# A macaron layer in split fp32: when blocks are fetched, where their splits stand in each queue, and who makes a few sums

## The chip, the cores and the metric

The kernel runs on one core of a Trainium2 chip. The metric is device time in microseconds of one execution. The five engines have queues of their own: TensorE (PE: matmuls, transposes), VectorE (DVE), ScalarE (ACT), GpSimd (POOL) and SyncE (SP). SyncE issues most loads and stores, GpSimd the DMAs that add to their destination.

## The reference

One layer, T = 1024 positions, width D = 1024, F = 2816:

```python
x = x + 0.5 * swiglu(rmsnorm(x, ffn1_norm), ffn1_w_in, ffn1_w_out)
x = x + hybrid_mixer(rmsnorm(x, mix_norm), ...)
x = x + 0.5 * swiglu(rmsnorm(x, ffn2_norm), ffn2_w_in, ffn2_w_out)
return rmsnorm(x, final_norm)

def swiglu(h, w_in, w_out):
    gate, up = split(h @ w_in, 2)
    return (silu(gate) * up) @ w_out
# mixer
za, zb, zg = split(h @ w_in, [2 * A, 2 * A + 3 * B])
u, v = split(gelu(za), 2)
v = einsum('hqp,bcphd->bcqhd', w_s, chunks_of_128(rmsnorm(v, sgu_norm))) + b_s
y_a = (u * v) @ w_proj_a
gate_b, gate_c, xb = split(zb, 3)
y_b = (gate_b * short_conv(gate_c * xb, conv_w)) @ w_proj_b     # width 3, by channel
return (sigmoid(g_a) * y_a + sigmoid(g_b) * y_b) @ w_out
```

All of it is float32.

## The kernel before

**Products.** Activations lie with features on the partitions and 512 positions (half the sequence, b = 0, 1) in a tile. Every float32 operand is split into a high part, rounded by a copy on ScalarE, and a low part, src - high on VectorE (`parts`, L87); a product of two operands is three matmuls: high x high, low x high and high x low. Over this lies a scheme with seven instead of eight block products: two output tiles (i = 0, 1) by two halves of the positions, the inner dimension cut in two parts of n tiles (n = 4, in short chunks 3 or 2). `group` makes one such unit: 84 matmuls of 128x512 for n = 4, in the order of products 1, 7, 6, 2, 5, 3, 4 (for n < 4: 1, 7, 6, 2, 5, 4, 3), with ScalarE copies t, u between them (L392), by which VectorE forms the four outputs, and `use` consumes these. `after(i)` is called behind product i and holds other work that shall stand there. `whole_terms` makes plain products, at the start and in two other groups.

**Names.** t1h, t1l ... t7h, t7l are the high and low parts of the seven sums of an activation block (`places`); wh and wl the parts of weights, wr the raw weights. Each weight of a group needs sums too: s2 = wr - wr and others by VectorE (L250, L251), for some weights by accumulating DMAs from GpSimd (`add_to`, L95); `make_ready`, `fetch_until` and `take` run through the list `plan` of all weights, some units ahead of the products. `fourth_sum` splits one of a weight's sums behind a ScalarE copy. gu, o, v, u, cx, gb, gg, ya and yb are the PSUM banks of the products (hidden layer in, layer out, the mixer's parts).

**Stages.** (1) x is loaded and transposed by feature (xT, `by_feature`), scaled by the norm's gain into hr and split; x itself is copied out to DRAM (xd). (2) FFN1: 22 gu groups; finished tiles go to DRAM as seven sums (`Shelf`, g and ts). (3) `out_chunks`: the chunks of FFN1 (4, 4 and 3 tiles twice) against the out weights, four o groups each, added to xd by DMA, the last chunk with the sum in SBUF (xl) and the squares for the next norm (`unhurried` holds these steps back). (4) Mixer: v groups, u groups with sgu (v's norm, `norm_v`; spatial product, `gate_heads`), cx/gb with the convolution, gg (gates), ya, yb, out. (5) FFN2 in the same way, with chunks of 4, 3 and 2 and four tiles (R) left over for (6): plain products o<-wah,gh with the final RMSNorm by token.

**Blocks from DRAM.** A `Shelved` block is fetched back from its shelf, one sum after another (`fetch`: n DMAs into a tile gr or mr, one for each k). Its constructor issues three fetches at once; each `make(i)` splits one sum and issues the next fetch. `last_group` calls `make` in its `after`, one product each, so the next chunk's block is split while the present chunk's last group runs.

**Order.** The scheduler of the Tile framework sets the order on each engine from priorities and the program's order; `tc.high_priority`, `tc.issue_after` and `issue_behind` (an edge without a semaphore) shift single instructions, and an instruction under `tc.keep_in_program_order` stays in the order of the code.

## Time and profile before

| | |
|---|---|
| median of three runs | 2173.31 us (2171.51, 2173.31, 4320.59) |
| profiled execution | 2174.83 us, span 2173.0 |
| TensorE busy | 2111.4 us, 97%, 9374 instructions, mean granted clock 0.99 |
| VectorE, ScalarE, GpSimd busy | 1367.6 (63%), 925.3 (43%), 420.5 (19%) |
| DMA | 435.98 MB, mean 201 GB/s |
| chain that ended last | PE 76%, DVE 7%, DMA 7%, issue 5%, ACT 4% |

The span runs from the first to the last instruction of the profiled execution; its own time is 1.8 us more. Of the run of twice the length there is no profile. Busy shares are means over all stages. The chain is the sequence of work that ended last, followed back from the end.

### The profile page before, as it was taken

To read this page: it belongs to the slowest core of one execution; us is meant where nothing else is said; L and a number is where in the kernel's file an instruction comes from. 1 tells how busy PE (TensorE), PEld (TensorE's weight loads), DVE (VectorE), ACT (ScalarE), POOL (GpSimd) and SP (SyncE) were. 2 spreads that over 40 slices of the span, in tenths; PEclk is the share of its full clock that TensorE was granted. 3 is DMA by queue.
4 is the path that set the end of the run, shared out by engine and by line. 5 is a ranking of instruction groups with operands and counts; after the bars stand their busy time and mean duration, and the time that the engine had idled before them with its cause. 6 is when DMAs were issued, how large, how long until landed. Compare 5 with 4: busy or idle time off the path is not lost.

```text
span 2173.0 us, 27092 instructions
## 1 busy us (share of the span) xinstructions
PE 2111.4 (97%) x9374; PEld 1737.5 (80%) x9374; DVE 1367.6 (63%) x1930; ACT 925.3 (43%) x1350; POOL 420.5 (19%) x486
## 2 busy tenths in 40 slices
PE   7999999999999989999999999999999999999987
PEld 6788888877877878888888888778888888888866
DVE  5855655676477446776654568587755655576666
ACT  5533333355366553222233535356433333354443
POOL 2011111112222111111111101212111111112313
PEclk8999999999999999999999999999999999999999
DMA  8487777979899646897798799867787777988962
GB/s 266 126 199 185 176 193 177 264 221 242 186 239 225 155 106 166 215 255 179 169 262 198 214 290 300 194 178 191 176 206 176 183 196 173 257 237 196 191 185 78
DMA packets 451247, 435.98 MB, mean 201 GB/s; under 512 B 26860, under 2 KB 313636, under 8 KB 451108
## 3 DMA queue, kind: packets, MB, share of 16 engines
q1 hardware_dynamic: 385604, 315.20, 45.4%
q0 software_dynamic: 65504, 119.04, 33.6%
q8 instruction: 73, 1.20, 0.2%
q14 instruction: 66, 0.54, 0.1%
HBM read 235.43 MB, written 100.66 MB: 155 GB/s over the span
## 4 chain that ended last, share of the span: by engine, by line
PE 76%; DVE 7%; DMA 7%; issue 5%; ACT 4%; SPq 1%; POOL 1%; DVEq 0%; POOLq 0%; ACTq 0%
PE gu L83 36%; PE o L83 14%; PE cx L83 7%; PE gg L83 7%; PE gb L83 4%; PE u L83 3%; PE v L83 2%; PE ya L83 2%; DMA gr<-g 1%; DMA wr<-in_ffn_w_out_dram 1%; DVE wl L87 1%; PE sgu L83 1%; PE yb L83 1%; DMA gr<-gd 1%; DMA wr<-wr 1%
## 5 line engine op out<-in xcount | busy, mean ns | idle before, releaser
L87 DVE TENSOR_TENSOR wl<-wr,wh 128x1024 fp32r<-128x1024 f32 (+3 forms) x420 | 441.5, 1054 | 524.9 <-ACT wh L87 516.7
L95 POOL DMA_DIRECT2D wr<-wr x342 | 297.2, 922 | 1489.2 <-DVE wl L87 705.2
L87 ACT CAST wh<-wr 128x1024 fp32r<-128x1024 f32 (+3 forms) x420 | 385.5, 921 | 338.4 <-PE gu L83 102.6
L392 ACT COPY u<-gu 128x512 f32<-128x512 f32 x82 | 47.9, 584 | 188.2 <-PE gu L83 188.2
L760 ACT ACTIVATE gu<-gu 128x512 f32<-128x512 f32 x88 | 55.0, 630 | 114.9 <-DVE gu L601 110.6
L99 DVE SCALAR_TENSOR_TENSOR gu<-gu,u 128x512 f32<-128x512 f32 x82 | 56.4, 688 | 46.7 <-PE gu L83 45.2
L601 DVE TENSOR_TENSOR gu<-gu,rb 128x512 f32<-128x512 f32 x120 | 78.9, 685 | 0.0
L95 POOL DMA_DIRECT2D xd<-o x64 | 56.5, 952 | 103.5 <-DVE o L99 35.3
L392 ACT COPY u<-o 128x512 f32<-128x512 f32 x54 | 31.4, 582 | 84.2 <-PE o L83 81.7
L83 PE MATMUL gu<-t1h,wh 128*128 128x512 f32 x180 | 50.5, 393 | 9.0 <-ACT t1h L87 9.0
L83 PE MATMUL gu<-t2l,wh 128*128 128x512 f32 x180 | 56.8, 390 | 1.6 <-DVE t2l L87 1.6
L83 PE MATMUL gu<-t2h,wh 128*128 128x512 f32 x180 | 57.5, 394 | 0.0
L763 DVE SCALAR_TENSOR_TENSOR gu<-gu,gu 128x512 f32<-128x512 f32 x88 | 57.2, 685 | 0.0
L83 PE MATMUL gu<-t2h,wl 128*128 128x512 f32 x180 | 56.7, 389 | 0.0
L392 ACT COPY t<-gu 128x512 f32<-128x512 f32 x41 | 24.1, 588 | 70.8 <-PE gu L83 70.8
L83 PE MATMUL gu<-t3h,wh 128*128 128x512 f32 x180 | 50.4, 392 | 1.6 <-ACT u L392 1.6
L83 PE MATMUL gu<-t5h,wh 128*128 128x512 f32 x180 | 50.4, 391 | 0.0
L83 PE MATMUL gu<-t1l,wh 128*128 128x512 f32 x180 | 50.2, 390 | 0.0
L83 PE MATMUL gu<-t3l,wh 128*128 128x512 f32 x180 | 50.1, 389 | 0.0
L83 PE MATMUL gu<-t1h,wl 128*128 128x512 f32 x180 | 50.1, 389 | 0.0
L83 PE MATMUL gu<-t5l,wh 128*128 128x512 f32 x180 | 50.1, 389 | 0.0
L83 PE MATMUL gu<-t3h,wl 128*128 128x512 f32 x180 | 50.1, 389 | 0.0
(630 smaller groups left out, 5122.8 us busy)
## 6 DMA issues: line engine op xcount, KB each, us to landing
wr<-wr POOLq DMA_DIRECT2D x318, 256.0 KB, 5.2
wr<-in_ffn_w_in_dram SPq DMA_DIRECT2D x258, 256.0 KB, 4.4
wr<-in_w_in_dram SPq DMA_DIRECT2D x166, 256.0 KB, 4.3
gr<-g SPq DMA_DIRECT2D x140, 256.0 KB, 5.5
g<-ts SPq DMA_DIRECT2D x80, 256.0 KB, 5.2
xd<-o POOLq DMA_DIRECT2D x64, 256.0 KB, 5.8
g<-gu SPq DMA_DIRECT2D x60, 256.0 KB, 4.8
wr<-in_ffn_w_out_dram SPq DMA_DIRECT2D x48, 256.0 KB, 4.4
```

Source lines behind the costliest of these rows:

```text
L83: return nc.tensor.matmul(ps, l, r, start=start, stop=stop, skip_group_check=more)
L87: return nc.scalar.copy(hi, src), nc.vector.tensor_tensor(lo, src, hi.bitcast(F32), ALU.subtract)
L95: nc.gpsimd.dma_start(dst, src, accum_op=ALU.add)
L99: nc.vector.scalar_tensor_tensor(dst, a, -1.0, b, ALU.mult, ALU.subtract)
L392: return nc.scalar.copy(*args)
L601: nc.vector.tensor_tensor(dst, dst, rb, ALU.mult)
L760: nc.scalar.activation(s, s, AF.Silu)
L763: nc.vector.scalar_tensor_tensor(s, s, 0.5, u, ALU.mult, ALU.mult)
```

## The change

- Start: ScalarE's table is loaded by a small copy at the top. Scaling (hr) and x copies are shared between ScalarE and VectorE, t1 and t2 are split in chunks of two tiles, and under `pin` the instructions stay in the code's order; the first half of group f = 0 is written out.
- `Shelved` issues no fetch when it is made; the callers call `fetch` once per group in the three groups ahead.
- Edges: the casts of blocks in `Shelved.make` get an edge behind the newest ScalarE copy u or t, and the low parts of sums 2, 3 and 4 one behind the newest low part of a weight. `unhurried` hands out four steps at a time at two places. u3 has no tile of its own.
- Short chunks (n < 4): one of the sums of a weight (s3, y + x) by VectorE; the same kind of edit for ya/yb: at d = 2 the sum with yb by VectorE.
- v's squares: half in the last v group, half in pairs in the first u group; `flush_v`, `norm_v` and the first `gate_heads` stand behind other products.
- End: remaining weights are fetched and split earlier, copies of xT are shared by ScalarE and VectorE.

```diff
     def parts(hi, lo, src):
-        return nc.scalar.copy(hi, src), nc.vector.tensor_tensor(lo, src, hi.bitcast(F32), ALU.subtract)
+        return pin(nc.scalar.copy(hi, src)), pin(nc.vector.tensor_tensor(lo, src, hi.bitcast(F32), ALU.subtract))
+    pinned = []
+    def pin(ins):
+        return tc.keep_in_program_order(ins) if pinned else ins
@@ make_ready
-                        parts(hi[:, :, :sz], lo[:, :, :sz], src[:, :, :sz])
+                        made = parts(hi[:, :, :sz], lo[:, :, :sz], src[:, :, :sz])
+                    newest_low[:] = [made[1]]
+                    if e == 2:
+                        issue_behind(made[0], newest_gain[0])
...
-                        add_to(y_[:, 0, :sz], x_[:, 0, :sz])
+                        if s[4] == KH:
+                            add_to(y_[:, 0, :sz], x_[:, 0, :sz])
+                        else:
+                            nc.vector.tensor_tensor(y_[:, 0, :sz], y_[:, 0, :sz], x_[:, 0, :sz], ALU.add)
@@ Blocks.make
-            parts(hi, lo, r[{1: (0, 0), 6: (0, 0), 7: (0, 1), 5: (0, 1), 2: (1, 0), 4: (0, 0), 3: (1, 1)}[i]])
+            src = r[{1: (0, 0), 6: (0, 0), 7: (0, 1), 5: (0, 1), 2: (1, 0), 4: (0, 0), 3: (1, 1)}[i]]
+            for c in range(0, z - a, 2):
+                q = min(c + 2, z - a)
+                parts(hi[:, c:q, :], lo[:, c:q, :], src[:, c:q, :])
@@ unhurried
-        for fn in todo_later:
+        now = todo_later[:4 if ins else None]
+        for fn in now:
...
-        todo_later.clear()
+        del todo_later[:len(now)]
@@ group
-                return nc.scalar.copy(*args)
+                newest_copy[:] = [nc.scalar.copy(*args)]
+            return newest_copy[0]
...
-        fourth_sum(copy(u2, ba))
+        third = copy(u2, ba)
+        unhurried(third)
+        fourth_sum(third)
...
-            u3 = act("u3")
-            tt(u3, bb_, u2, ALU.add)
+            tt(u2, bb_, u2, ALU.add)
...
+    nc.scalar.copy(small("table", 1), ones[:, 0:1])
@@ by_feature
+            if both and d % 2:
+                pin(nc.vector.tensor_scalar(blk.raw[c, b][:, d % KH, :], ps, gain(0, d), None, ALU.mult))
+            else:
+                newest_gain[:] = [pin(nc.scalar.mul(blk.raw[c, b][:, d % KH, :], ps, gain(0, d)))]
+            def keep_x(d=d, ps=ps):
+                xs = act("x")
+                if both and d % 2 == 0:
+                    pin(nc.scalar.copy(xs, ps))
+                else:
+                    pin(nc.vector.tensor_copy(xs, ps))
+                nc.gpsimd.dma_start(xd[d][b], xs)
@@ first_groups
-        by_feature(0, range(KH))
-        blk.make(1)
+        pinned.append(True)
+        keep = by_feature(0, range(KH), True)
+        blk.make(1, 0, 2)
+        make_ready(at[0] + 1)
+        blk.make(1, 2, KH)
         ws.append(take(2, 0))
+        for fn in keep:
+            fn()
...
+        for m in range(3):
+            for i in range(2):
+                for k in range(KH):
+                    w = ws[0][i][m == 2][:, 0, k * P:(k + 1) * P]
+                    mm(banks[0][i, 0], w, blk.at(1, k)[m == 1], m == k == 0, False)
+            if m == 0:
+                keep = by_feature(0, range(KH, ND), True)
+                blk.make(2, 0, 2)
+                blk.make(2, 2, KH)
+        pinned.clear()
@@ Shelved
-            for _ in range(3):
-                self.fetch()
...
+            behind = list(newest_low) if i in (2, 3, 4) else []
...
-                parts(hi, lo, src)
+                high, low = parts(hi, lo, src)
+                issue_behind(high, newest_copy[0])
+                for other in behind:
+                    issue_behind(low, other)
@@ swiglu_in (the same in out_chunks from d == 0, in gg from d == ND - 4 and in ya from d == 0)
-            if f == NF - 3:
+            if f == NF - 4:
                 nxt = Shelved(shelves[0], "g")
+            if NF - 4 <= f < NF - 1:
+                nxt.fetch()
@@ v and u
+    def squares_v(c, ts):
+        for t in ts:
+            junk = act("junk")
+            nc.scalar.activation(junk, v[t // TPB, c][:, t % TPB, :], AF.Square,
+                                 accum_out=ssqv[:, c * NT + t:c * NT + t + 1])
+    PAIRS = {6: (0, 1), 5: (2, 3), 2: (4, 5), 3: (6, 7)}
...
+            if hd == 6 and i in PAIRS:
+                squares_v(0, PAIRS[i])
...
-            if hd == 0 and i == 2:
+            if hd == 0 and i == 7:
                 flush_v()
+            if hd == 0 and i in PAIRS:
+                squares_v(1, PAIRS[i])
+            if hd == 0 and i == 4:
                 norm_v()
-            if hd > 0 and i == 6:
+            if hd > 0 and i == (2 if hd == 1 else 6):
                 gate_heads()
@@ yb and the end
-            if d < KH - 1:
+            if d < KH - 2:
                 add_to(y, sl[i, b])
...
-        group("o", blk, use)
+        group("o", blk, use, after=lambda i: fetch_until(len(plan)) if i == 5 else None)
...
-                nc.scalar.copy(xt[b, c][:, j, :], ps[j])
+                (nc.vector.tensor_copy if j % 2 else nc.scalar.copy)(xt[b, c][:, j, :], ps[j])
```

Three places in the order of instructions. In these rows a number behind a name tells tiles of the same name apart. ScalarE at the very start, before:

```order
1 L87 ACT_TABLE_LOAD
2 L87 CAST wh_266<-wr_103 128x1024
3 L87 CAST wh_276<-wr_106 128x1024
4 L619 ACTIVATE hr_137<-xT_226,gains 128x512
5 L619 ACTIVATE hr_137<-xT_235,gains 128x512
6 L619 ACTIVATE hr_137<-xT_244,gains 128x512
7 L619 ACTIVATE hr_137<-xT_253,gains 128x512
8 L87 CAST t1h_262<-hr_137 128x2048
9 L87 CAST t6h_280<-wr_270 128x1024
```

and now:

```order
1 L519 ACT_TABLE_LOAD
2 L519 COPY table_82<-ones 128x1
3 L646 ACTIVATE hr_139<-xT_228,gains 128x512
4 L646 ACTIVATE hr_139<-xT_240,gains 128x512
5 L87 CAST t1h_252<-hr_139 128x1024
6 L87 CAST wh_256<-wr_105 128x1024
7 L87 CAST t1h_252<-hr_139 128x1024
8 L87 CAST wh_268<-wr_108 128x1024
9 L651 COPY x_272<-xT_228 128x512
```

The table load moved from behind the weight's arrival to the top, t1h is cast in two pieces around the first weight, and two of the four scalings and two copies of x went from one engine to the other.

VectorE in the last gu group, before (wl_3623 and wl_3633 are weights of the first o group, t2l, t3l, t4l its blocks):

```order
383 L87 TENSOR_TENSOR wl_3623<-wr_3439,wh_3622 128x1024
384 L601 TENSOR_TENSOR gu_3649<-gu_3649,rb_835 128x512
385 L601 TENSOR_TENSOR gu_3667<-gu_3667,rb_831 128x512
386 L87 TENSOR_TENSOR t2l_358<-gr_3555,t2h_357 128x1024
387 L598 TENSOR_TENSOR gu_3687<-gu_3535,rb_835 128x512
388 L87 TENSOR_TENSOR t3l_516<-gr_3617,t3h_515 128x1024 x2
389 L250 TENSOR_TENSOR wr_3757<-wr_3593 128x512
390 L99 SCALAR_TENSOR_TENSOR gu_3708<-gu_3536,u_653_3533 128x512
391 L87 TENSOR_TENSOR wl_3633<-wr_3581,wh_3632 128x1024
392 L87 TENSOR_TENSOR t4l_726<-gr_3656,t4h_725 128x1024 x2
```

and now, with the same two weights as wl_3639 and wl_3649:

```order
384 L621 TENSOR_TENSOR gu_3683<-gu_3683,rb_847 128x512
385 L618 TENSOR_TENSOR gu_3703<-gu_3551,rb_851 128x512
386 L87 TENSOR_TENSOR wl_3639<-wr_3455,wh_3638 128x1024
387 L105 SCALAR_TENSOR_TENSOR gu_3724<-gu_3552,u_654_3549 128x512
388 L260 TENSOR_TENSOR wr_3778<-wr_3609 128x512
389 L87 TENSOR_TENSOR wl_3649<-wr_3597,wh_3648 128x1024
390 L87 TENSOR_TENSOR t2l_319<-gr_3571,t2h_318 128x1024 x2
391 L87 TENSOR_TENSOR t3l_522<-gr_3633,t3h_521 128x1024 x2
392 L621 TENSOR_TENSOR gu_3724<-gu_3724,rb_847 128x512
393 L87 TENSOR_TENSOR t4l_740<-gr_3672,t4h_739 128x1024
```

The second weight's low part moved from behind t2l and t3l to a place ahead of both.

ScalarE in the first u group and the start of the second, where the squares (junk) were 16 in a row; the last part of these before:

```order
492 L957 ACTIVATE junk_6501,ssqv_6482<-v_5502 128x512
493 L994 ACTIVATE u_6442<-u_6442 128x512
494 L957 ACTIVATE junk_6503,ssqv_6482<-v_5502 128x512
495 L87 CAST wh_6412<-wr_6100 128x1024
496 L957 ACTIVATE junk_6505,ssqv_6482<-v_5502 128x512
497 L957 ACTIVATE junk_6507,ssqv_6482<-v_5504 128x512
498 L957 ACTIVATE junk_6509,ssqv_6482<-v_5504 128x512
499 L957 ACTIVATE junk_6511,ssqv_6482<-v_5504 128x512
500 L957 ACTIVATE junk_6513,ssqv_6482<-v_5504 128x512
501 L392 COPY t_1271_6588<-u_6591 128x512
502 L994 ACTIVATE u_6569<-u_6569 128x512
```

and now the last three pairs:

```order
492 L87 CAST wh_6444<-wr_6115 128x1024
493 L409 COPY u_1223_6379<-u_6380 128x512
494 L987 ACTIVATE junk_6513,ssqv<-v_5514 128x512
495 L987 ACTIVATE junk_6515,ssqv<-v_5514 128x512
496 L87 CAST wh_6479<-wr_6118 128x1024
497 L987 ACTIVATE junk_6527,ssqv<-v_5516 128x512
498 L987 ACTIVATE junk_6529,ssqv<-v_5516 128x512
499 L1065 ACTIVATE u_6509<-u_6509 128x512
500 L987 ACTIVATE junk_6546,ssqv<-v_5516 128x512
501 L1065 ACTIVATE u_6523<-u_6523 128x512
502 L987 ACTIVATE junk_6548,ssqv<-v_5516 128x512
503 L87 CAST wh_6489<-wr_6121 128x1024
```

The squares stand in pairs between the copies u, the gelus (u<-u) and the weights, the first eight of them in an earlier group. TensorE there, where sgu is v's spatial product, before:

```order
1201 L83 MATMUL u_6592<-t7h_714,wl_6403 128x512 x4
1202 L83 MATMUL u_6591<-t6h_280,wh_6412 128x512 x4
1203 L83 MATMUL u_6591<-t6l_281,wh_6412 128x512 x4
1204 L83 MATMUL u_6591<-t6h_280,wl_6413 128x512 x4
1205 L83 MATMUL sgu_6650<-wsT_5500,v_5504 128x128
1206 L83 MATMUL sgu_6659<-wsT_5499,v_5501 128x128 x4
```

and now:

```order
1197 L83 MATMUL u_6613<-t2h_318,wh_6444 128x512 x2
1198 L83 MATMUL u_6613<-t2l_319,wh_6444 128x512 x2
1199 L83 MATMUL u_6613<-t2h_318,wl_6445 128x512 x2
1200 L83 MATMUL sgu_6714<-wsT_5512,v_5516 128x128
1201 L83 MATMUL sgu_6723<-wsT_5511,v_5513 128x128 x4
1202 L83 MATMUL sgu_6714<-wsT_5512,v_5516 128x128 x3
```

sgu stood behind product 6 of the second u group, and now stands behind products 6, 2 and 5 of it.

## Rows read from the trace of the kernel before

**Rows 1.** Stretches: busy us (instructions) of PE, PEld, DVE, ACT, POOL; clock; DMA share.

```profile
150.00:200.00 50.00, 50.00 (x222) 41.42 (x221) 28.94 (x41) 16.42 (x24) 8.72 (x10) 1.00 0.81 198
...
440.00:466.00 26.00, 23.28 (x99) 17.81 (x97) 26.00 (x31) 20.67 (x25) 2.45 (x3) 1.00 0.64 192
...
780.00:812.00 32.00, 25.24 (x117) 21.07 (x116) 17.57 (x41) 20.31 (x57) 4.29 (x5) 0.89 0.42 99
...
2060.00:2080.00 20.00, 15.54 (x59) 12.30 (x58) 11.00 (x21) 5.24 (x10) 4.27 (x5) 0.83 0.75 171
...
2160.00:2173.00 13.00, 0.47 (x3) 0.04 (x1) 6.03 (x26) 3.96 (x9) 3.13 (x3) 0.61 0.32 122
```

**Rows 2.** TensorE's waits, grouped: total us, times, longest.

```profile
PE gu L83 <- ACT t1h L87: 9.0, 1, 9.0
PE o L83 <- ACT wah L87: 5.2, 1, 5.2
PE o L83 <- ACT wh L87: 4.5, 1, 4.5
PE sgu L83 <- DVE v L964: 4.4, 1, 4.4
PE o L83 <- ACT u L392: 4.4, 9, 1.1
PE o L83 <- DVE wl L87: 4.3, 4, 2.8
PE yb L83 <- ACT t L392: 2.3, 1, 2.3
PE v L83 <- DVE wl L87: 2.0, 1, 2.0
PE u L83 <- ACT t L392: 2.0, 1, 2.0
```

**Rows 3.** ScalarE in time at the start: start, duration, instruction [idle before].

```profile
9.42 1.28 ACT L87 ACT_TABLE_LOAD   x1 [9.42 <-DMA wr<-in_ffn_w_in_dram]
10.72 1.99 ACT L87 CAST wh<-wr 128x1024 fp32r<-128x1024 f32 x2
12.61 2.42 ACT L619 ACTIVATE hr<-xT,gains 128x512 f32<-128x512 f32 x4
15.06 1.90 ACT L87 CAST t1h<-hr 128x2048 fp32r<-128x2048 f32 x1
```

**Rows 4.** TensorE in time at the start.

```profile
17.01 1.22 PE L83 MATMUL gu<-t1h,wh 128*128 128x512 f32 x2 [9.01 <-ACT t1h L87]
...
38.83 0.50 PE L83 MATMUL gu<-t1h,t6h 128*128 128x512 f32 x1 [0.19 <-DVE x L621]
```

**Rows 5.** VectorE in time at the end of the last gu group.

```profile
464.83 1.21 DVE L87 TENSOR_TENSOR wl<-wr,wh 128x1024 fp32r<-128x1024 f32 x1
```

**Rows 6.** SyncE's queue in time from 470 to 496.

```profile
477.50 12.18 SPq L740 DMA_DIRECT2D gr<-g  x12
```

**Rows 7.** The chain of waits from 470 to 510.

```profile
494.32 10.52 DMA wr<-in_ffn_w_out_dram
```

**Rows 8.** VectorE in time, 668 to 680.

```profile
675.74 0.69 DVE L388 TENSOR_TENSOR u<-o,u 128x512 f32<-128x512 f32 x1 [4.16 <-DMA xd<-xl]
```

**Rows 9.** ScalarE in time, 784 to 812.

```profile
785.68 0.77 ACT L957 ACTIVATE junk<-v 128x512 f32<-128x512 f32 x1
```

**Rows 10.** VectorE in time, 784 to 812.

```profile
800.35 6.43 DVE L964 TENSOR_SCALAR v<-v,y 128x512 f32<-128x512 f32 x16
```

**Rows 11.** ScalarE in time, in three places from 1386 on.

```profile
1395.52 1.47 ACT L87 CAST t1h<-mr 128x1536 fp32r<-128x1536 f32 x1 [5.59 <-DMA mr<-sl]
...
2071.73 1.14 ACT L87 CAST wh<-wr 128x512 fp32r<-128x512 f32 x2 [7.24 <-DMA wr<-wr]
...
2114.00 3.95 ACT L87 CAST wah<-wr 128x1024 fp32r<-128x1024 f32 x4
```

**Rows 12.** VectorE in time, 2058 to 2074.

```profile
2057.88 0.42 DVE L250 TENSOR_TENSOR wr<-wr 128x256 f32<-128x256 f32 x1
```

More of the change, by code (lines that the diff above doesn't have):

```diff
@@ L427, in group @@
             product(4, bd)
-            use(1, 0, bd, u3)
+            use(1, 0, bd, u2)
             after(4)
@@ L608, in load, with by_feature @@
         return t
+    newest_gain = []
     blk = Blocks("h")
-    def by_feature(b, ds):
+    def by_feature(b, ds, both=False):
+        keep = []
         for d in ds:
@@ L618, in by_feature @@
                 nc.tensor.transpose(ps[:, j * P:(j + 1) * P], xin[b, c][:, j, o:o + P], ident)
-            nc.scalar.mul(blk.raw[c, b][:, d % KH, :], ps, gain(0, d))
-            xs = act("x")
-            nc.vector.tensor_copy(xs, ps)
-            nc.gpsimd.dma_start(xd[d][b], xs)
+            if both and d % 2:
[9 more added lines that the diff above has]
+                nc.gpsimd.dma_start(xd[d][b], xs)
+            if both:
+                keep.append(keep_x)
+            else:
+                keep_x()
+        return keep
     def rstd_of_x(b):
@@ L648, in half @@
             for f in range(2):
-                for i in range(2):
-                    banks[f][i, b] = bank("gu")
                 for j in range(2):
-                    if f == 0 and j == 1 and b == 0:
-                        by_feature(0, range(KH, ND))
-                        blk.make(2)
+                    if j == 0:
+                        if f == b == 0:
+                            continue
+                        for i in range(2):
+                            banks[f][i, b] = bank("gu")
                     for k in range(KH):
@@ L659, in half @@
                 if f == 0 and b == 0:
-                    by_feature(1, range(ND))
-        by_feature(0, range(KH))
-        blk.make(1)
-        ws.append(take(2, 0))
+                    for fn in by_feature(1, range(ND), True):
+                        fn()
[4 more added lines that the diff above has]
+        blk.make(1, 2, KH)
+        ws.append(take(2, 0))
+        for fn in keep:
+            fn()
+        for i in range(2):
+            banks[0][i, 0] = bank("gu")
+        for m in range(3):
+            for i in range(2):
+                for k in range(KH):
[6 more added lines that the diff above has]
+        pinned.clear()
+        for fn in keep:
+            fn()
         ws.append(take(2, 0))
@@ L822, in use @@
                         add_to(xd[e][b], o)
-                if d == KH - 2 and not last:
+                if d == 0 and not last:
                     nxt = Shelved(shelves[ch + 1], "g")
+                if d < KH - 1 and not last:
+                    nxt.fetch()
                 if d < KH - 1:
@@ L952, in norm_v @@
     def norm_v():
-        ssqv = small("ssqv", 2 * NT)
-        for c in range(2):
-            for t in range(NT):
-                junk = act("junk")
-                nc.scalar.activation(junk, v[t // TPB, c][:, t % TPB, :], AF.Square,
-                                     accum_out=ssqv[:, c * NT + t:c * NT + t + 1])
         sv = small("sv", NT)
@@ L1079, in use @@
             nc.sync.dma_start((sad, sbd)[i][d][b], s)
-        if d == ND - 3:
+        if d == ND - 4:
             nxt = Shelved(ad, "a")
+        if ND - 4 <= d < ND - 1:
+            nxt.fetch()
         if d < ND - 1:
@@ L1103, in use @@
             nc.sync.dma_start(pad[d + i * KH][b], sl[i, b])
-        if d == KH - 2:
+        if d == 0:
             nxt = Shelved(bd, "b")
+        if d < KH - 1:
+            nxt.fetch()
         if d < KH - 1:
@@ L1193 @@
     out_chunks(blk, shelves, CHUNKS2, use_last, finish)
+    ws = take(NF - LAST)
     xt = {(b, c): xs[c, b] for b in range(NB) for c in range(2)}
@@ L1208 @@
         nc.gpsimd.tensor_scalar(fg[c], fg[c], -0.125, None, ALU.mult)
-    ws = take(NF - LAST)
     def add(ps, t, c):
```

4 lines of the change are left out of this document (3 added, 1 removed).

## Prediction

> **What bounds the kernel now.** I read the stretches of time first. Where nothing disturbs it, TensorE runs 222 matmuls of 128x512 in 50 us without a gap, 0.225 us each, at a granted clock of 1.00 (2.4 GHz) [rows 1]. The change keeps every matmul and transpose, so that time stays, and only what TensorE loses can be won. Of the span of 2173.0 us its busy time is 2111.4, so it stands for 61.6 us; some 12.5 of these lie at the end, in the final norm, which the change leaves alone (the last 13 us of the span hold 0.47 of TensorE [rows 1]). To the idle time comes the slow clock: two stretches with a long gap show 0.83 and 0.89 [rows 1], that is, TensorE ran part of them at its half clock (1.2 GHz).
>
> Second, TensorE's waits [rows 2]. The row of a wait names the last releaser. Four single waits of 4.4 to 9.0 us make 23 us; the rest are short ones, mostly on ScalarE's copies of a bank (t, u) or VectorE's low part of a weight (wl). Third, for each wait, the releaser's engine: is it late because its own input was late, or because of what stands ahead of it in its queue? Both occur, and the change treats them differently.
>
> **The start.** ScalarE waits for a weight until 9.42, then loads its table (1.28), casts two weights (1.99), scales the four transposed tiles (2.42) and casts t1h for all four (1.90) [rows 3]; TensorE gets its first product at 17.01, and the product with t6h as a weight, f=1, begins at 38.83 [rows 4]. In the new order the load stands ahead of everything and hides under the input's DMA. The transposes end at about 8; ScalarE and VectorE then scale two tiles each (2 x 0.6, to 9.3), ScalarE casts half of t1h (0.95, to 10.3) and then the weight (1.0, to 11.2). So TensorE starts at about 11.2 instead of 17.0, with half of the product. Behind that it has the same work. From 17.01 to 38.83 were 21.8 us; it now also meets the second weight's cast (13.1). I let 1.2 of the 5.8 be lost there and win 2.4 from t2 in halves and the x copies that two engines share: **-7.0**. Bounds: -4 if f=1's weights, cast late on ScalarE, decide; -9.5 if no wait remains.
>
> At this place a page has another figure. The row shows 1.28 for the load and the next instruction 0.02 behind it. The Trainium skill, "ScalarE: Activation LUTs", section "What ACT_TABLE_LOAD costs", gives 1283 ns for the load and about 1380 ns more for a drain, 2.66 us in all. The trace agrees with the first and shows no drain here. By the page the term would be -8.4.
>
> **Edges between groups.** In the last gu group the low part wl stands behind t3l in VectorE's queue and starts at 464.83 [rows 5]; TensorE waits for it 1.04. It could not start earlier, since VectorE is busy for 26.00 of the 26 us from 440 to 466 [rows 1]. The new order puts this and the next wl ahead of t2l and t3l, and ScalarE's u ahead of the casts of t5h. A moved split costs nothing if it still meets its product: behind wl (ends at about 460) the two t2l and two t3l are 4.6 us, so t2l is there at 462.3; its product is the fourth of the next group, 3 x 12 matmuls x 0.225 = 8.1 us after that group begins (456.8 unstalled), at 464.9. That is 2.6 us of cover, thin, and it is the reason for a residue below. The same cure reaches the edges at o, u, gg, ya and yb. Of the 4.4 us in nine waits o<-u [rows 2] I take 3.5, because u now stands ahead of the casts at most of these edges.
>
> The largest o<-wl, 2.8 of 4.3, is another thing: that wl needs a weight whose DMA was issued only after twelve block fetches in a row, 12.18 us for the twelve, and whose own DMA took 10.52 behind them [rows 6, 7]. With one block per group four of these twelve go earlier, and one block comes behind the weights; at about 1 us per fetch in the queue the weight is 8 us sooner. -2.8; with the 1.04 above and small ones **-4.0** for the row. Where the fetches go instead, the queue gets four more at a time in a group whose weights are otherwise early (no wait there now).
>
> The 2.0 of v<-wl: VectorE stood 4.16 us before adding u3, because the tile u3 came from the pool of act tiles and waited for the DMA xd<-xl; the wl is queued behind it [rows 8]. Now the add goes into u2, no tile is asked for: **-2.0**. Edges together: 3.5 + 4.0 + 2.0 = **-9.5**. The nine rows of [rows 2] make 38.1 us; with the 12.5 at the end they leave 11 of the 61.6 for small waits of under 2 us, most of the same kinds. I take **-4.4** of these, between 0 and -8.
>
> **v's squares and norm.** ScalarE does the 16 squares in one run, the first at 785.68 and one every 0.6 us with a few other steps between [rows 9], the copy t of the next group behind them (TensorE waits 2.0); VectorE is through with the root at 800.35, about 2.6 us behind the last square, and does 16 scalings in 6.43 us [rows 10], and sgu waits 4.4 and runs at the half clock behind it. The new order has the first 8 squares in the v group before, the other 8 in pairs after products 6, 5, 2 and 3 of u's first group, and sgu three products later in the next. The last pair, behind product 3, is done near 789.5; the root by 793; the scalings, with weights' low parts between, by 801. sgu's place is 5 products behind 790.3, at 803.8. So 2.8 us of cover: 4.4 + 2.0 and the half clock go. For the clock, 0.89 over 32 us [rows 1] bounds the loss at 0.11 x 32 = 3.5, which holds some of the gap itself; I take 2.9. **-9.3**, and 0 to -9.7 as bounds; if the scalings are 3 us later than I think, 0.2 is lost again.
>
> **Adds taken from DMA.** In the short chunks the cast of a weight waited 7.24 us for an accumulating DMA [rows 11], which cost TensorE 4.5; now VectorE adds, at 0.42 us for 128x256 [rows 12]; while ScalarE waits, VectorE has nothing to do either. 0.83 over 20 us [rows 1] bounds the slow clock at 3.4, I take 2.5: **-7.0**. For yb, t1h waited 5.59 for the same kind of DMA, with the copy t behind it [rows 11]; the add at d=2 goes to VectorE: 2.3 of TensorE's time [rows 2], and for the clock 1.4, an estimate by the two gaps above (2.9 behind 4.4, 2.5 behind 4.5, about 0.6 per us): **-3.7**.
>
> **The last stretch.** The wait for wah, 5.2. ScalarE had two gh, 16 copies of 0.5 and then wah at 2114.00 [rows 11]. Half of the copies go to VectorE and wah stands ahead of the last of them; the second gh still waits for its DMA at 2108.4. Then gh (1.8), two copies (1.0), wah at 2111.2 and ready at 2112.2 instead of 2115: **-3**, between -1 and -5.
>
> **The sum.** 7.0 + 9.5 + 4.4 + 9.3 + 7.0 + 3.7 + 3 = 43.9. Against this stands what the trace can't show, new stalls: some hundred moved instructions at about a dozen edges, with 2 to 3 us of cover at the two that I worked out. I allow 2 us, and 4 at worst, where everything moved lies beside other work. 43.9 - 2 = 42: the profiled execution took 2174.83, so 2132.8 by its own time, and from the median of 2173.31, 1.5 below it, **2131**. A difference of 2% would be 43.5 us, 2129.8; that is about what can be told from no change, and the forecast lies at its edge.
>
> **Rivals.** (1) *All goes*: the bounds of the start, the small waits and the last stretch come in at their far ends (9.5, 8, 5), without new stalls: 43.9 + 2.5 + 3.6 + 2 = 52, or 2121. For it speaks that most of these waits come from the order in a queue alone, and that ScalarE is busy for 43% and VectorE for 63% of the span. Against it: VectorE has no pause at such an edge [rows 1]. (2) *The edges move their waits*: t2l, t3l and t4l now stand behind the newest wl; where that weight is late, TensorE waits for a block instead. Then the 9.5 and the 4.4 of small waits are not won, and the start gives only 4: 43.9 - 13.9 - 3.0 = 27, or 2146. The same time comes out if the order at the edges does not do what it says because inputs decide. (3) *Slower*: the fetches of one block per group hold SyncE's queue. A fetch waits for a free buffer or for its turn on the queues, and a weight stands behind it; eight blocks' sets are fetched like this, three fetches each, so 24 places. What one such hold does is seen at 505 [rows 6, 7]: a weight 10.5 us behind, TensorE 2.8 us idle. It decides from 42 / 24 = 1.75 us of wait per place; with the 2.8 it is 24 x 2.8 = 67 us of loss against 42 of gain, or 2198. Against it: the edges have the buffers free, since the blocks of the chunk in use are split before its first group.
>
> **Chances.** The forecast (2125 to 2137) 0.40, rival 1 (2115 to 2125) 0.28, rival 2 (2137 to 2156) 0.28, rival 3 0.04. The range leaves out rival 3 and the ends of the other two: 2116 to 2153. Faster by over 2%: rival 1 and 0.4 of the forecast's span, 0.28 + 0.16 = 0.44; slower: rival 3, 0.04; within 2%: the rest, 0.52.
>
> **What would show it.** Right: the first gu matmul at 11 to 12 and f=1 at 31 to 33; no wait of TensorE over 2 us between the start and the last stretch; sgu without a wait and at full clock; no wait on wr<-wr or mr<-sl; wah near 2112 on the old scale. Wrong: waits on t2l, t3l or t4l at the edges (rival 2), SyncE's weights behind block fetches with wl named as releaser in the middle of groups (rival 3), or f=1 still held by t6h.

## The result and the profile after

The changed kernel took 2140.76 us (median of 4 runs, 2136.95 to 2142.77), the kernel before 2176.11 (median of 4) on the same chip. One of those four is the run of 4320.59; the median of the other three is 2173.31, so 32.6 us lie between the medians, and the ratio, which leaves that run out, is 0.984, with an interval from 0.982 to 0.986. The forecast was 2131 with a range from 2116 to 2153: the time lies inside the range, but beyond the stretch from 2125 to 2137 that the prediction calls the forecast. It is also within the 2% that the prediction named as most likely.

The profiled execution took 2139.29 us, of which the span is 2137.5; before it was 2173.0, so the two spans differ by 35.5 where the forecast had 42. The page's first part, busy time by engine, and the first line of its chain:

```profile
PE 2099.5 (98%) x9374; PEld 1733.7 (81%) x9374; DVE 1385.6 (65%) x1979; ACT 922.9 (43%) x1368; POOL 410.6 (19%) x470
...
PE 81%; issue 6%; DMA 6%; DVE 3%; ACT 2%; POOL 1%; SPq 0%; POOLq 0%; ACTq 0%; DVEq 0%
```

TensorE's idle time within the span fell from 61.6 to 38.0 us (2137.5 less 2099.5), and its busy time by 11.9 us, since less of it runs at the half clock (the mean granted clock rose from 0.990 to 0.994). TensorE's waits, grouped as in [rows 2]:

```profile
PE o L83 <- DVE wl L87: 6.8, 3, 4.8
PE gu L83 <- ACT wh L87: 2.9, 1, 2.9
PE o L83 <- ACT wah L87: 2.6, 1, 2.6
PE xT L642 <- ACT gu L384: 1.9, 1, 1.9
PE o L83 <- ACT u L409: 1.8, 2, 1.6
```

Of the nine rows of [rows 2], those for t1h, wh at o, v at sgu, wl at v, and the two for t are gone. One has grown: o<-wl, from 4.3 to 6.8. In the place of the 9.0 at the start stand two new ones, gu<-wh and xT<-gu. The stretches of time, in the columns of [rows 1]:

```profile
440.00:466.00 26.00, 26.00 (x117) 21.44 (x116) 26.00 (x31) 17.18 (x22) 3.87 (x5) 1.00 0.75 205
460.00:480.00 20.00, 20.00 (x90) 16.57 (x89) 11.52 (x17) 7.28 (x10) 5.18 (x6) 1.00 1.00 267
480.00:500.00 20.00, 15.19 (x64) 12.22 (x64) 6.51 (x8) 3.45 (x5) 5.25 (x6) 0.94 0.99 249
750.00:800.00 50.00, 50.00 (x249) 42.19 (x248) 30.08 (x57) 33.16 (x81) 8.74 (x10) 1.00 0.58 123
2020.00:2040.00 20.00, 19.08 (x84) 15.49 (x83) 18.01 (x28) 12.31 (x19) 5.17 (x6) 1.00 1.04 269
2123.50:2137.50 14.00, 0.00 (x0) 0.00 (x0) 6.24 (x27) 5.01 (x11) 3.79 (x3) 0.58 0.30 113
```

Read them against [rows 1]. The stretch from 440 to 466 has no gap, with VectorE as full as before. It holds less of the last gu group than before, since TensorE now enters the first o group at 448.01 instead of 458.54; but ahead of 440 there is no gap either, and the new order is as the prediction had it: t2l is through at 453.93, and its product begins at 456.24, so 2.3 us of cover (forecast 2.6). The norm of v (750 to 800) has TensorE busy throughout at a clock of 1.00, where 780 to 812 had 25.24 of 32 at 0.89. The stretch of the short chunks (now 2020 to 2040) has 19.08 of 20 at full clock against 15.54 at 0.83. What is bad is 480 to 500: 15.19 of 20. And the end is longer: TensorE's last matmul now stands 14.0 us ahead of the last instruction (12.6 before).

For a balance I took, in both traces, the time from each matmul's start to the next one's, less 0.227 us for a 128x512 and 0.110 for a 128x128, and summed what is over by place. It counts gaps and the slow clock together. The row of edges is what remains of the whole.

| place | before, us | after, us | won | forecast |
|---|---|---|---|---|
| start, 0 to 50 | 18.5 | 11.9 | 6.6 | 7.0 |
| edges and small waits, except the next row | 23.4 | 10.9 | 12.5 | 11.1 |
| the late weight (505 before, 493.6 after) | 3.1 | 7.8 | -4.7 | 2.8 |
| v's squares, norm, sgu | 11.1 | 1.0 | 10.1 | 9.3 |
| yb | 4.3 | 0.1 | 4.2 | 3.7 |
| adds in the short chunks | 7.1 | 1.2 | 5.9 | 7.0 |
| last stretch | 7.6 | 5.2 | 2.4 | 3.0 |
| after the last matmul | 12.6 | 14.0 | -1.4 | 0 |
| allowance for new stalls | | | in the rows | -2.0 |
| sum | | | 35.6 | 42 |

The sum agrees with the 35.5 of the spans. So most terms came in at their size, and one of them has the wrong sign.

The start, TensorE and then ScalarE in time (with two later places of ScalarE), each with start, duration, instruction and the idle time before it:

```profile
11.63 2.17 PE L83 MATMUL gu<-t1h,wh 128*128 128x512 f32 x4 [2.91 <-ACT wh L87]
...
31.29 1.15 PE L642 MATMUL xT<-ident,xin 128*128 128x128 f32 x8 [1.88 <-ACT gu L384]
32.26 0.47 PE L83 MATMUL gu<-t1h,t6h 128*128 128x512 f32 x1
```

```profile
0.72 1.28 ACT L519 ACT_TABLE_LOAD   x1 [0.72 <-PEq L1349]
2.01 0.19 ACT L519 COPY table<-ones 128x1 f32<-128x1 f32 x1
...
28.55 1.04 ACT L87 CAST t6h<-wr 128x1024 fp32r<-128x1024 f32 x1 [3.87 <-DMA wr<-in_ffn_w_in_dram]
...
651.39 0.59 ACT L409 COPY u<-o 128x512 f32<-128x512 f32 x1 [2.22 <-DMA xd<-xl]
...
2074.88 1.90 ACT L87 CAST gh<-gr 128x2048 fp32r<-128x2048 f32 x1 [2.94 <-DMA gr<-gd]
```

The first product comes at 11.63 (forecast 11 to 12) and f=1 at 32.26 (31 to 33); what is left there is a weight whose DMA lands at 28.5, with ScalarE's cast t6h behind it. The row at 651.39 is a wait that moved: the tile that u3 no longer asks for [rows 8] is asked for by another step of the same pool, here a copy of u, 2.22 us. TensorE waits for that copy:

```profile
652.03 0.97 PE L83 MATMUL o<-t3h,wh 128*128 128x512 f32 x3 [1.56 <-ACT u L409]
```

This is most of the row o<-u above. The row at 2074.88 shows that the final wait still hangs on the DMA gr<-gd.

### The profile page after: what moved, and what is told of

Same layout as the page of the kernel before. It is cut to its first block, busy times and chain, and to the rows that moved or that the text cites. A ratio compares the mean times of both kernels' runs of the same rounds, so it can differ in the third digit from the quotient of the medians.

```text
span 2137.5 us, 27134 instructions
## 1 busy us (share of the span) xinstructions
PE 2099.5 (98%) x9374; PEld 1733.7 (81%) x9374; DVE 1385.6 (65%) x1979; ACT 922.9 (43%) x1368; POOL 410.6 (19%) x470
## 4 chain that ended last, share of the span: by engine, by line
PE 81%; issue 6%; DMA 6%; DVE 3%; ACT 2%; POOL 1%; SPq 0%; POOLq 0%; ACTq 0%; DVEq 0%
PE gu L83 38%; PE o L83 11%; PE cx L83 7%; PE gg L83 7%; PE u L83 4%; PE yb L83 4%; PE gb L83 4%; PE ya L83 3%; PE v L83 2%; DMA wr<-in_ffn_w_out_dram 1%; DMA wr<-wr 1%; DMA wr<-in_ffn_w_in_dram 1%; POOL xd L101 1%; DMA gr<-g 1%; PE sgu L83 1%
## 5 line engine op out<-in xcount | busy, mean ns | idle before, releaser
L101 POOL DMA_DIRECT2D wr<-wr x330 | 289.9, 936 | 1480.1 <-DVE wl L87 663.1
L83 PE MATMUL gu<-t5h,wl 128*128 128x512 f32 x180 | 50.1, 389 | 0.0
```

The lines of the kernel that those rows point to most:

```text
L83: return nc.tensor.matmul(ps, l, r, start=start, stop=stop, skip_group_check=more)
L101: nc.gpsimd.dma_start(dst, src, accum_op=ALU.add)
```

## The experiments

Each is a small edit of the kernel before or of the changed one. Waits are quoted as TensorE's instruction behind the wait.

**The norm part alone** (e1_norm_only): the squares, their PAIRS and the later place of sgu, put into the kernel before.

```
+    PAIRS = {6: (0, 1), 5: (2, 3), 2: (4, 5), 3: (6, 7)}
...
+            if hd == 6 and i in PAIRS:
+                squares_v(0, PAIRS[i])
...
-        ssqv = small("ssqv", 2 * NT)
-        for c in range(2):
-            for t in range(NT):
-                junk = act("junk")
...
-            if hd == 0 and i == 2:
+            if hd == 0 and i == 7:
...
+            if hd == 0 and i in PAIRS:
+                squares_v(1, PAIRS[i])
+            if hd == 0 and i == 4:
...
-            if hd > 0 and i == 6:
+            if hd > 0 and i == (2 if hd == 1 else 6):
...
```

> The kernel before with one part of the change alone: v's squares in pairs, the norm and the first sgu later. My theory (each edit removes its own wait, independent of the others): the wait u<-t (2.0), sgu<-v (4.4) and the half clock behind it go, 9 to 10 us or 0.5%: ratio 0.9955, and TensorE has no wait over 0.5 us between 770 and 812. Rival (the squares only move, so ScalarE is late for the casts of weights in the last v group and u's first group instead): 0 to 4 us of gain, ratio 0.998 to 1.0, with waits on ACT wh or u in those two groups.

It took 2166.46 against 2176.12, a ratio of 0.996 (0.9945 to 0.9975): 9.7 us. The stretch that answers to the third row of [rows 1] (10 us wider):

```profile
770.00:812.00 42.00, 42.00 (x211) 35.62 (x210) 25.82 (x52) 25.89 (x62) 6.94 (x8) 1.00 0.59 130
```

No gap, full clock. The term of 9.3 stands by itself. In the changed kernel the rows show the cover: VectorE's scalings, and TensorE's sgu behind them without a wait, 2.4 us after they end (forecast 2.8).

```profile
784.85 6.42 DVE L1035 TENSOR_SCALAR v<-v,y 128x512 f32<-128x512 f32 x16
...
495.18 0.69 DVE L260 TENSOR_TENSOR wr<-wr 128x512 f32<-128x512 f32 x1 [10.26 <-DMA wr<-in_ffn_w_out_dram]
```

The second row is from another place, and belongs to the next question.

**Why the weight at 493 is late: three fetches at once again** (e2_three_fetches). VectorE stands 10.26 us for this weight's DMA, and TensorE behind it. Either the new order on SyncE's queue holds the weight, or the DMAs have no more to give. The edit puts the fetches back in threes, where the kernel before had them.

```
+            for _ in range(3):
+                self.fetch()
...
-            if f == NF - 4:
+            if f == NF - 3:
-            if NF - 4 <= f < NF - 1:
-                nxt.fetch()
...
```

> The changed kernel with blocks fetched three at once again, two groups ahead of the chunk that needs them, as before the change. In the changed kernel the wait at the second group of FFN1's out chunk grew from 2.78 us to 4.81 and half a clock behind it (7.8 us of loss against 3.1). Theory A (order in SyncE's queue: the block fetch of the first group, which the change put there, stands ahead of that group's weights): with the fetches back at their old place this wait falls to 0 to 3 us and the kernel is 4 to 7 us faster than the changed one, near 2134, ratio 0.981. Theory B (the DMAs of this stretch are at their throughput, which order doesn't change): the loss stays at 5 to 8 us here, time within 2 us of the changed kernel, ratio 0.984. Theory C (the spread helps elsewhere): other waits of 3 us and more come back, ratio above 0.986.

It took 2140.18, ratio 0.983 (0.9815 to 0.985), as the changed kernel; and the wait stayed, first in the changed kernel, then here:

```profile
498.38 2.07 PE L83 MATMUL o<-t6h,wl 128*128 128x512 f32 x4 [4.81 <-DVE wl L87]
```

```profile
500.22 2.08 PE L83 MATMUL o<-t6h,wl 128*128 128x512 f32 x4 [3.93 <-DVE wl L87]
```

The 3.93 lies within what executions with the new order show (2.3 to 4.8, below). So the explanation by the order of the fetches falls, and with it the step of the prediction that expected to win from that order.

**The same place with fewer bytes** (e6_no_xd): the four accumulating DMAs xd of the first o group are left out, so that this part of the sum is missing.

```
-                        add_to(xd[e][b], o)
+                        if (ch, d, chunks) != (0, 0, CHUNKS1):
+                            add_to(xd[e][b], o)
```

> The changed kernel without the eight... of four adding DMAs per group: the four sums of the first output group of FFN1 are not added to x (that part of the result is left out, all else is computed). The wait near 493 was 4.81, 3.93, 2.20 and 2.42 us in four kernels that differ little there. Theory A (the DMAs between 455 and 500 are at their throughput): with 4 of some 20 transfers of that group gone, the weight lands 3 to 5 us sooner and the wait is 0 to 1 us. Theory B (order in SyncE's queue, where the weights stand behind block fetches): GpSimd's adds are another queue, the wait stays at 2 to 5 us.

One run, 2134.37. The stretch from 460 to 500:

```profile
460.00:500.00 40.00, 40.00 (x178) 33.14 (x177) 19.91 (x26) 12.83 (x18) 6.97 (x8) 1.00 0.94 258
```

TensorE has no gap, and VectorE has the weight 8.6 us sooner (495.18 in the changed kernel):

```profile
486.57 0.69 DVE L260 TENSOR_TENSOR wr<-wr 128x512 f32<-128x512 f32 x1 [2.05 <-DMA wr<-in_ffn_w_out_dram]
```

The weight's fetch stands on SyncE's queue, the four transfers on GpSimd's; with them gone it is issued 3.2 us sooner (479.84 for 483.01), its transfer takes less than 6.8 us instead of 12.05, and it is in time. So the other transfers under way held the weight, on its way and in SyncE's queue. In the changed kernel's chain of waits three transfers of some 10 us each stand there, each issued 0.02 us behind the landing of the one before:

```profile
463.69 10.00 DMA wr<-in_ffn_w_out_dram
473.69 0.02 issue
473.71 9.28 DMA gr<-g
482.99 0.02 issue
483.01 12.05 DMA wr<-in_ffn_w_out_dram
```

The share of the DMA engines is a rough sign of this and no more: over 460 to 500 it is 1.00 in the changed kernel and 0.94 here, with 258 GB/s in both, and the kernel before has 1.10 and 302 GB/s from 480 to 500 (shown further down).

**How steady this wait is** (e9_after_again, e12_after_third): the changed kernel without an edit, on two more chips.

> The changed kernel once more, unaltered, beside the two below. If the size of the wait near 493 (4.81 us in the first profile, 2.2 to 3.9 in kernels that differ little there) is a matter of one execution's DMA timing, this profile shows another value, 2 to 5 us, at the same instruction, and the median stays within 0.2% of 2140.76 (ratio 0.982 to 0.986). If it belongs to the kernel, it is 4.5 to 5 us again.

> The changed kernel a third time, one look. Up to the wait near 493 its instructions stand in the same order as in two of the kernels above (adds by DMA, norm by VectorE), whose waits there were 2.42 and 2.43 us; its own were 4.81 and 4.59. If the size is set by something that differs from execution to execution, a value between 2 and 5 us, as likely near 2.4 as near 4.7; if it goes with the kernel after all, 4.5 to 4.9 a third time.

e9 took 2138.02 (5 runs), ratio 0.983 (0.980 to 0.985), with a wait of 4.59; e12, one run of 2137.37, had

```profile
496.18 1.21 PE L83 MATMUL o<-t6h,wl 128*128 128x512 f32 x4 [2.60 <-DVE wl L87]
```

The executions of the changed kernel and of its variants that leave fetches and edges as they are: 4.81, 4.59, 2.69 (e11), 2.63 (e8), 2.60, 2.43 (e10), 2.42 (e4) and 2.27 (e7). Three with the order of before: 2.78, 2.61 (e1) and 2.59 (e5). So in most executions the wait is what it was, and in two of eight it is 2 us longer. In those two the weight's own transfer took 12.05 and 12.04 us from issue to landing, in the six others 9.8 to 10.6. By the balance above, with the half clock behind the wait, the place cost 7.8 us in these two, 4.5 to 4.6 in e8, e11 and e12, and 2.5 to 2.7 in e4, e7 and e10; before, e1 and e5 it cost 3.1, 2.9 and 4.3. Why the transfer takes 10 or 12 us, and what decides about the clock, stays open.

**Without the edges** (e3_no_edges): the two orderings of splits at a group's edge are taken out.

```
-                issue_behind(high, newest_copy[0])
-                for other in behind:
-                    issue_behind(low, other)
```

> The changed kernel without the two edges in the split of a fetched block (behind the newest ScalarE copy, and behind the newest low part of a weight). My theory: the waits on u and wl at the groups in which blocks are split come back: 2.8 at the end of gu, about 1 to 1.5 each at the ends of the out chunks, of gg and ya and in FFN2, together 8 to 10 us; ratio 0.988 to 0.989. Rival (the other edits, with more of VectorE and ScalarE free, already put these splits right): 0 to 2 us, ratio 0.984 to 0.985.

It took 2147.13, ratio 0.987 (0.9855 to 0.989): 6 us slower than the changed kernel's 2140.76, 9 than its 2138.02 in e9, and 6 to 7 than e4 and e2 of its own series. That is at or under the lower end of my 8 to 10, and far more than the rival's 0 to 2. Its waits:

```profile
PE o L83 <- DVE wl L87: 5.8, 6, 2.2
PE o L83 <- ACT u L409: 4.0, 7, 1.4
```

The row o<-u is back at 4.0 in 7 waits (4.4 in 9 in [rows 2]; 1.8 in 2 in the changed kernel), and wl has 6 waits instead of 3. The edges do what they say, at u above all. The last gu group, for which the prediction worked out the order of t2l and t3l, has lost only 0.7 of TensorE here (25.33 of the 26 us from 440 to 466), so the other parts of the change had cured most of it already.

**The adds in the short chunks, by DMA again** (e4_adds_by_dma), and **alone in the kernel before** (e5_adds_only).

```
-                        if s[4] == KH:
-                            add_to(y_[:, 0, :sz], x_[:, 0, :sz])
-                        else:
-                            nc.vector.tensor_tensor(y_[:, 0, :sz], y_[:, 0, :sz], x_[:, 0, :sz], ALU.add)
+                        add_to(y_[:, 0, :sz], x_[:, 0, :sz])
```

> The changed kernel with the sum of weights in the short chunks by an accumulating DMA again. My theory: the 7 us DMA comes back ahead of the cast of the weight in the last out chunk of FFN2, TensorE waits 4 to 5 us there and 2 to 3 us of slow clock follow: 7 us, ratio 0.9875. Rival (that wait came from the order of GpSimd's queue, where the DMA stood behind the stores xd, and this order is another one now): 0 to 2 us, ratio 0.984 to 0.985.

> The kernel before with one part alone: in the short chunks the sum of a weight is made by VectorE. Theory A (a DMA that adds is late there because it stands in GpSimd's queue behind the stores xd; a sum on VectorE avoids that queue, so this part is enough by itself): no wait of 4.5 us near 2068, 5 to 7 us faster, ratio 0.997. Theory B (the weight is late for another reason, the other edits removed the wait): the wait stays at 3 to 5 us, ratio 0.999 to 1.001.

e4 took 2141.33, ratio 0.984 (0.982 to 0.986), and the wait of 4.5 did not come back:

```profile
2020.00:2040.00 20.00, 19.42 (x86) 15.75 (x85) 17.70 (x27) 10.23 (x17) 6.91 (x8) 1.00 1.03 263
```

e5 took 2168.87 against 2176.73, ratio 0.996 (0.995 to 0.9975), 7.9 us, and has no gap at the place of before:

```profile
2060.00:2080.00 20.00, 20.00 (x90) 16.58 (x89) 18.55 (x35) 7.76 (x14) 3.41 (x4) 1.00 0.90 227
```

So the adds by VectorE are enough alone, as the prediction had it, but in the changed kernel they aren't needed. What else differs there is GpSimd's queue. In the kernel before, the adding DMA (wr<-wr) stands behind three sums of o into xd; in e4 it stands ahead of two of them (the orders of the two programs):

```
before:
395 L95 DMA xd_25_136<-o_2840_16349 128x512
396 L95 DMA xd_24_135<-o_2842_16364 128x512
397 L95 DMA xd_17_128<-o_2843_16378 128x512
398 L95 DMA wr_2829_16290<-wr_2828_16287 128x256
e4:
391 L101 DMA xd_26_138<-o_2832_16393 128x512
392 L101 DMA wr_2822_16335<-wr_2821_16332 128x256
393 L101 DMA xd_25_137<-o_2834_16408 128x512
394 L101 DMA xd_18_130<-o_2835_16422 128x512
```

The 7.24 us that ScalarE waited [rows 11] did not by themselves cost TensorE its 4.5. The DMA took about as long from issue to landing in both, 7.2 before and 6.6 in e4. But VectorE's step that it needs ended at 2058.30 [rows 12] before and the DMA was issued at 2064.46, 6.2 us later; in e4 these are 2024.28 and 2025.88, 1.6 us. These 4.6 us of place in the queue, behind sums that wait for a product, are about the wait that went. That is read from these rows and was not tried by itself.

**The table** (e7_no_table): the early copy that loads ScalarE's table is left out.

```
-    nc.scalar.copy(small("table", 1), ones[:, 0:1])
```

> The changed kernel without the small copy that loads ScalarE's table at the top. By the rows (1.28 us for the load and 0.02 behind it) ScalarE's first scaling starts 1.3 us later and the first product at 12.9 instead of 11.6. By the Trainium skill (ScalarE: Activation LUTs, What ACT_TABLE_LOAD costs: 2.66 us with the drain) it would be 14.3. Rival: the load is placed early in any case, and nothing changes.

One run, 2132.74, too few to tell a time from it; the first gu matmul is at 11.49 instead of 11.63. ScalarE at the start:

```profile
4.46 1.28 ACT L645 ACT_TABLE_LOAD   x1 [4.46 <-DVE gains L540]
8.30 1.27 ACT L645 ACTIVATE hr<-xT,gains 128x512 f32<-128x512 f32 x2 [2.56 <-PE xT L641]
```

The load now belongs to the scaling of hr, which comes first in the new order, and has been through for 2.56 us when the transposes are ready. In the kernel before it hung on a cast that waited for a weight until 9.42 [rows 3]. The copy is worth nothing here; the order of ScalarE's first steps moved the load under cover. In the changed kernel the step behind the load starts at 2.01, and the load ends at 2.00: as in [rows 3], the row shows no drain. By the figure of the Trainium skill ("ScalarE: Activation LUTs", section "What ACT_TABLE_LOAD costs") nothing would change either, as an estimate, since 1.38 us more lie within the 2.56.

**All of these adds by VectorE** (e8_all_adds_dve): the branch shown with e4 without its condition.

```
-                        if s[4] == KH:
-                            add_to(y_[:, 0, :sz], x_[:, 0, :sz])
-                        else:
-                            nc.vector.tensor_tensor(y_[:, 0, :sz], y_[:, 0, :sz], x_[:, 0, :sz], ALU.add)
+                        nc.vector.tensor_tensor(y_[:, 0, :sz], y_[:, 0, :sz], x_[:, 0, :sz], ALU.add)
```

> The changed kernel with this sum by VectorE in the long chunks and the projections too, not only in the short chunks: 20 adding DMAs fewer, 20 VectorE instructions of 0.68 us more. Theory A (throughput of the DMAs decides the wait near 493): less traffic there, the wait falls to 0 to 2 us; 2 to 4 us faster than the changed kernel, ratio 0.982 to 0.983. Theory B (order decides, and VectorE is full at the edges): wait as before, and 0 to 2 us of new waits on wl at the edges; ratio 0.984 to 0.986.

It took 2134.97, ratio 0.980 (0.979 to 0.982), while the wait at the late weight stayed at 2.63. It is between 3 and 6 us under the changed kernel's medians on other chips; e11 below shows how little of that is its own.

**The final norm by VectorE** (e10_norm_by_dve), and **both** (e11_both, e8 and e10 together). The product of gain and root, until now one multiply on GpSimd and one on ScalarE or VectorE, becomes one step of VectorE.

```
-            nc.gpsimd.tensor_tensor(xg[c], xt[t // TPB, c][:, t % TPB, :], fg[c], ALU.mult)
...
-            if c == 0 or t < NT - 1:
-                nc.scalar.mul(xt[t // TPB, c][:, t % TPB, :], xg[c], y)
-            else:
-                nc.vector.tensor_scalar(xt[t // TPB, c][:, t % TPB, :], xg[c], y, None, ALU.mult)
+            nc.vector.scalar_tensor_tensor(xt[t // TPB, c][:, t % TPB, :], xt[t // TPB, c][:, t % TPB, :], y, fg[c], ALU.mult, ALU.mult)
```

> The changed kernel with the final norm's two multiplications (gain, root) in one VectorE instruction of 0.7 us per 512 columns, none on GpSimd and ScalarE. In the changed kernel the last matmul ends 14.0 us before the end (12.6 before the change), and a step of VectorE of 128x1 takes 1.28 us instead of 0.16 while GpSimd multiplies. Theory A (VectorE's round of 5.55 us per 128 positions, longer than TensorE's 5.45, sets the end; GpSimd's multiplication holds it up): from the last matmul to the end 9 to 11 us, the short steps 0.16 to 0.25, 3 to 4 us faster than the changed kernel. Theory B (the end is set by the last store and the chain of the last tile alone): 12 to 14 us as now, 0 to 1 us.

> The kernel before this one, and in addition all sums of this kind of weights by VectorE (as in the run with all adds on VectorE, ratio 0.9804). If both gains are real and independent: 7 to 9 us faster than the changed kernel beside it, ratio near 0.979. If the adds' gain was scatter between chips: 3 to 4 us.

In one series of 5 runs each with e9 (2136.44 to 2140.55), e10 took 2133.37 (2130.29 to 2134.86), ratio 0.981 (0.978 to 0.984), 4.7 us less, and the runs don't overlap. From the last matmul's end to the span's end are now 8.7 us instead of 14.0:

```profile
2119.80:2128.50 8.70, 0.00 (x1) 0.00 (x0) 4.97 (x16) 0.72 (x2) 0.00 (x0) 0.65 0.33 121
```

VectorE in the root's last steps, first in the changed kernel, then in e10:

```profile
2126.90 1.25 DVE L1325 SCALAR_TENSOR_TENSOR z<-q,z 128x1 f32<-128x1 f32 x1
...
2128.44 0.16 DVE L1325 SCALAR_TENSOR_TENSOR z<-q,z 128x1 f32<-128x1 f32 x1
```

```profile
2123.49 0.16 DVE L1323 SCALAR_TENSOR_TENSOR z<-q,z 128x1 f32<-128x1 f32 x1
2123.68 1.41 DVE L1326 SCALAR_TENSOR_TENSOR xs<-xs,z,fg 128x512 f32<-128x512 f32 x2
```

The same step of one element per partition takes 0.16 or 1.25 us. How much of the 4.7 comes from these short steps, and how much from the steps and hand-overs that fell away with the multiplies, no run tells apart. e11 took 2131.90 (2129.61 to 2133.12), ratio 0.980 (0.9775 to 0.982): 1.5 less than e10, with overlapping runs. So e8's gain is some 1.5 by this series and can't be told from nothing, and the rest of its distance to the changed kernel lies within what separates series on different chips. e11 has the lowest median of the kernels with several runs, 44 us under the kernel before and 6 under the changed one.

## Why the prediction was right, and where not

**Right by its terms.** The start, 6.6 for 7.0, is confirmed at both of its marks (11.63, 32.26). The edges and small waits without the late weight gave 12.5 for 11.1, and e3 shows that 6 to 9 of these come from the ordering itself; how the rest divides over other parts (halves of splits, the steps handed out by fours) is not shown. The norm gave 10.1 for 9.3, and 9.7 alone (e1). yb gave 4.2 for 3.7, the last stretch 2.4 for 3.0. The start, yb and the last stretch were not tried by themselves; there the rows bear the cause out, and no run does.

**The step that failed** is "at about 1 us per fetch in the queue the weight is 8 us sooner". It counted the queue's issue time alone, and set the weight against TensorE's old place. The weight was in fact issued 11.3 us sooner (483.01 for 494.32 [rows 7]). But TensorE now comes to this product 11.8 us sooner (493.6 for 505.4), since it wins time ahead of it, and the transfer took 12.05 instead of 10.52. Together these make the wait 2.0 longer, 4.81 for 2.78. The 10.52 in [rows 7] should have warned: the queue had issued the transfer, and it was slow among others, in a stretch that was as full before:

```profile
480.00:500.00 20.00, 20.00 (x90) 16.55 (x89) 7.23 (x9) 6.12 (x9) 5.17 (x6) 1.00 1.10 302
```

e2 shows no gain from the order of the fetches, and e6 that four transfers fewer remove the wait. Instead of 2.8 won, 4.7 were lost in the profiled execution: the term is 7.5 us off, more than the 6.3 by which the whole sum was short, and that the other misses nearly cancel is luck. In six of the seven other executions above the place costs 2.5 to 4.6 against 3.1 before, so even there it wins 0.6 at best. For this scatter the prediction had no term.

**Smaller misses.** The 2.0 for u3 ("no tile is asked for") came to little: the wait for a tile moved to the copy of u at 651.39, and TensorE waits 1.56 for it. The end after the last matmul, which the prediction says the change "leaves alone", took 1.4 more. The code of the norm is unchanged, and the slow 128x1 step was there before as well (1.26 at 2162.36). VectorE's rounds per 128 positions settle at 5.5 to 5.6 us in both, where TensorE needs 5.44; but the first sum of the stage starts later, 11.2 us behind the stage's first matmul (2078.75) instead of 9.1 (2115.17), and waits for TensorE in both, first in the changed kernel, then before:

```profile
2089.98 1.37 DVE L1305 TENSOR_TENSOR xs<-o,xs 128x512 f32<-128x512 f32 x2 [5.14 <-PE o L83]
```

```profile
2124.24 0.69 DVE L1228 TENSOR_TENSOR xs<-o,xs 128x512 f32<-128x512 f32 x1 [4.46 <-PE o L83]
```

Why TensorE has the first product of this stage later is not shown. That the stage's end hangs on VectorE's and GpSimd's steps is shown by e10. The adds gave 5.9 for 7.0: the time came as forecast, but the adds bring it alone (e5), and so do the other edits without them (e4), so counting both would have been double. The table's 1.3 us came from the order and not from the copy (e7). The allowance of 2 for new stalls was met by rows that the balance holds: the 1.56 at 652.03, and a new wait of 1.62 for wl at 1412, where the balance of 1400 to 1575 rose to 6.1 from 4.3 in the same work before (1422 to 1597):

```profile
1412.49 0.74 PE L83 MATMUL o<-t7h,wl 128*128 128x512 f32 x2 [1.62 <-DVE wl L87]
```

**The signs.** The norm's came (sgu without a wait, full clock), and so did that of wah: its first cast starts 1.5 us behind the last transpose, which is 2111.5 on the old scale (near 2112). Two did not: a wait of 4.81 stands between the start and the last stretch, and ScalarE still waits for wr<-wr, 9.8 us in six waits, the longest 2.8 (14.4 and 7.2 before).

**The rivals.** The time lies in rival 2's stretch (from 2137), but not by its mechanism: no wait is on t2l, t3l or t4l. Its second reading, that inputs decide at an edge, fits one place, the late weight. Rival 3 spoke of weights behind fetches; its sign, wl named in the middle of a group, did appear, at 493.6, where e2 speaks against the fetches as the cause, and at 1412, which was not tried. Rival 1 needed three far ends, of which two did not come: 6.6 for 9.5 at the start and 2.4 for 5 in the last stretch.

## What to carry to other kernels

When an engine waits for a weight, look at how long the weight's own transfer takes, and at what else is under way, before the queue is reordered: here another order of the fetches won nothing, and four transfers fewer removed the wait. And a forecast that wins time ahead of such a place has to bring the weight sooner by as much, only to keep the wait as it is. Before an accumulating DMA is given to another engine, its place in GpSimd's queue is worth a look: here a place ahead of two other sums went with the same gain. And a long run of side work on one engine, like the sixteen squares, is best cut in pairs and given to the groups ahead of the point where it is needed.

## What was not expected of the hardware

VectorE's step on 128x1 took 1.25 us instead of 0.16 when it began 0.03 us behind GpSimd's multiply, which lasted as long. GpSimd in time in the changed kernel:

```profile
2126.87 1.26 POOL L1309 TENSOR_TENSOR xg<-xs,fg 128x512 f32<-128x512 f32 x1 [1.75 <-issue]
```

The Trainium skill, "SBUF — State Buffer", section "SBUF: two separate sides", says that VectorE and GpSimd share a pair of ports as an exclusive lock, kept for a whole instruction, and that steps of VectorE with two inputs in SBUF take part. The rows agree: the step with z and q as inputs ended with GpSimd's (2128.15 and 2128.13), and without GpSimd's multiplies (e10) every such step took 0.15 to 0.22.

The clock behind a gap of 2 to 3 us came out both ways. Four matmuls behind the late weight took 1.20 us, full clock, after gaps of 2.78 (before) and 2.61 (e1), and those behind them kept it. After 2.59 (e5) the four took 2.08, half clock. After 2.60 (e12) they took 1.21, and the clock fell to half 1.3 us behind their start. After the shortest gap of these, 2.20 (e3), it fell as well (1.78 for the four). The length of the gap alone did not decide it in these rows.
